# Feed-forward, up: eight products for the two leading chunks, two of five operand blocks made first

## The chip, the cores and the metric

The kernel runs on one core of one Trainium2 chip. The metric is the device time of one execution in microseconds (us); the median of three runs is compared. A core has TensorE (PE, matmuls out of SBUF into the PSUM banks), VectorE (DVE), ScalarE (ACT), GpSimd (POOL, which works on SBUF only here) and SyncE (SP, which issues the DMA transfers here). Each takes its instructions in a fixed order and waits for the others by semaphores.

## What is computed

Two transformer blocks in a row over 1024 tokens of width 1024, all in float32. The change is in the second block, between the output projection of its attention and the feed-forward part:

```python
x = x + gate1 * (merged @ w_out[i])
h2 = rmsnorm(x, g_ffn[i]) * (1 + scale2) + shift2
u = depthwise_conv_seq(h2 @ w_up[i], conv_w[i], conv_b[i])
u_val, u_gate = jnp.split(u, 2, axis=-1)
x = x + gate2 * ((jax.nn.gelu(u_gate, approximate=True) * u_val) @ w_down[i])
```

`w_up` has 1024 rows and 5632 columns, 2816 for `u_val` and 2816 for `u_gate`. `depthwise_conv_seq` has three taps along the tokens. `rmsnorm` needs the sum of squares of each token over all 1024 channels.

## The kernel before

Channels lie on the 128 partitions, tokens along the free dimension, in two halves of 512. Each float32 operand of a matmul is split into a high and a low part in a reduced format (`split_sb`: a copy on ACT makes the high part, a subtraction on DVE or POOL the low part), and a product takes three matmuls (high x high, high x low, low x high) for each block of 128 channels.

**Output projection.** `dense` goes over the tiles `mt` 0 to 7 in two groups of four, first token half, then second. `evac` (L1635) adds the residual (`stt` into `X3[th][:, mt]`), stores it, and `squares` adds up the squares in `acc[th]` (in the trace `ac`; `X3` and its slices are `x`, as is the residual's source). When the first half is complete (`after`, i = 12), `rstd_rows` makes the factor of each token: column sums by PE (`rs`), a power on POOL (`rbv`), transposes by PE (`rb`, a PSUM tile). The first half is then modulated and split into the operand blocks B11 (channels 0 to 511) and B21 (512 to 1023). When the second half is complete, a second `rstd_rows` (L1659) follows for `acc[1]`, out of the PSUM pool `o2ps`, which is then closed. The PSUM pool `upps` (six banks `u`) opens after it.

**Feed-forward, up.** There are 22 chunks `f`. Chunk f makes 128 channels of `u_val` (tile f) and 128 of `u_gate` (tile f + 22) for both token halves: a 2 x 2 by 2 x 2 block product. The weight blocks are a11, a12 (value, lower and upper channels) and a21, a22 (gate); the operand blocks B11, B21 (first token half) and B12, B22 (second). It is done with seven block products instead of eight, with sums of weight blocks (`weights`: `z` and `s4`, four DVE operations, split by `split_w`) and sums of operand blocks T1 = B12 - B11, T2 = B22 - T1, T3 = B12 - B22, T4 = T2 - B21. Each block product is 12 matmuls of 128x512 (`prod`, L1701 to L1707), a chunk 84. Then DVE adds the products together, ACT and DVE apply the taps, ACT the gelu, and the result goes to HBM (`a_d`).

The first two chunks are done together, since they come when T1, T2, T3, T4 and B22 are not there yet: `first` and `first2` for both (B11 and B21 products, 48 matmuls), then the loop over k = 0 to 3 (L1801 on), which modulates the second half and makes the five blocks for that k in one go, T1 and T3 and B22 with the low part on POOL, T2 and T4 on DVE, and then `up([0, 1])`, whose three first products go k by k. From chunk 2 on `up([f])` does one chunk after another.

**Order.** The program is written in the order of the source. A planner (a list scheduler with a model of the engines) then orders each engine's instructions: among those that are ready in its model it takes the one that stands first in the source. A PSUM bank or an SBUF tile is used again when its last reader is done. The pool `w2` (`a0`, `a1`, `r2`, `p5`, `cg`) takes the 32 KB per partition of X3[0] and, behind it, X3[1]; its tiles are laid out in the order of their first use in the source, in this kernel `p5`, `cg`, `a0`, `a1`, `r2`. The weights come by `raw` (L1671): tile f into `wst` (two buffers), tile f + 22 into `r2` (two buffers, trace name `r`), except for the first two chunks, where all come into `wst`. Split weights have four buffers (`wh`, `wl`).

Of the kernel before, what the change touches and what calls it, by code (L numbers as in the profile page):

```python
# [10 lines left out]
F32 = mybir.dt.float32  # L11
# [40 lines left out]
class Kernel:  # L52
# [1520 lines left out]
    def block2b(self):  # L1573
# [85 lines left out]
        rb = self.rstd_rows([acc[1]], D, 1e-6, t_, pp, "n", 2)  # L1659
# [11 lines left out]
        def raw(f, g, joint):  # L1671
            p, t = (w2, "r2") if g and not joint else (self.wp, "wst")
# [4 lines left out]
        def weights(f, joint):  # L1677
# [32 lines left out]
        P, P2 = {}, {}  # L1710
        K4 = range(4)

        def first(f, joint=False):

            gen = weights(f, joint)
            w = split_w(next(gen))
            a = bank()
            p1 = w1.tile([128, 512], F32, name="p1", tag="p1", bufs=2)
            cv = w1.tile([128, 1024], F32, name="cv", tag="cv", bufs=2)
            P[f] = gen, a, p1, cv, w  # L1720
            prod(a, w, 0, B11, K4, True)
            self.act(p1, a, AF.Copy)

        def first2(f, joint=False):
            gen, a, p1, cv, w = P[f]
            if joint:
                a = P2[f] = bank()
            prod(a, w, 1, B21, K4, joint)
            if not joint:
                self.act(cv[:, :512], a, AF.Copy)  # L1730

        W, b, c, d = {}, {}, {}, {}

        def up_weights(f):
            W[f] = [split_w(next(P[f][0])) for _ in range(2)]

        def up(fs):
            for f in fs:
                if f not in P:
                    first(f)  # L1740
            joint = len(fs) > 1
            for f in fs:
                if f not in W:
                    W[f] = [split_w(next(P[f][0]))]
                b[f] = bank()
                if not joint:
                    prod(b[f], W[f][0], 0, T2, K4, True)
                    first2(f)
                if len(W[f]) < 2:
                    W[f].append(split_w(next(P[f][0])))  # L1750
                c[f] = bank()
                if not joint:
                    prod(c[f], W[f][1], 0, T1, K4, True)
            if joint:
                for f in fs:
                    d[f] = bank()
                for k in K4:
                    for f in fs:
                        prod(b[f], W[f][0], 0, T2, [k], True)
                        prod(c[f], W[f][1], 0, T1, [k], True)  # L1760
                        prod(d[f], W[f][1], 1, T4, [k], True)
            for f in fs:
                gen, a, p1, cv, w = P.pop(f)
                if joint:
                    self.tt(cv[:, :512], p1, P2[f], ALU.add)
                self.tt(cv[:, 512:], p1, b[f], ALU.add)
                p5 = w2.tile([128, 512], F32, name="p5", tag="p5", bufs=2)
                self.act(p5, c[f], AF.Copy)
                cg = w2.tile([128, 1024], F32, name="cg", tag="cg", bufs=2)
                prod(b[f], W[f][0], 1, T3, K4, False)  # L1770
                self.tt(cg[:, 512:], p1, b[f], ALU.add)
                if not joint:
                    d[f] = bank()
                    prod(d[f], W[f][1], 1, T4, K4, True)
                self.tt(cg[:, :512], cg[:, 512:], d[f], ALU.subtract)
                self.tt(cg[:, 512:], cg[:, 512:], p5, ALU.add, eng=nc.gpsimd)
                w = split_w(next(gen))
                prod(c[f], w, 0, B22, K4, False)
                self.tt(cv[:, 512:], cv[:, 512:], c[f], ALU.add)
                a = []  # L1780
                for g, u in enumerate((cv, cg)):
                    mt = f + NFF * g
                    x = w2.tile([128, 1024], F32, name=f"a{g}", tag=f"a{g}", bufs=2 - g)
                    self.act(x, u, AF.Identity, bias=self.vec("conv_b", mt), scale=wc(1, mt))
                    self.stt(x[:, 1:], u[:, :1023], wc(0, mt), x[:, 1:], ALU.mult, ALU.add)
                    self.stt(x[:, :1023], u[:, 1:], wc(2, mt), x[:, :1023], ALU.mult, ALU.add)
                    a.append(x)
                self.act(a[1], a[1], AF.Gelu_apprx_tanh)
                self.tt(a[0], a[0], a[1], ALU.mult)
                nc.sync.dma_start(self.a_d[f], a[0])  # L1790


        db = w1.tile([128, 4], F32, name="db")
        self.tt(db, self.ada[:, 24:28], self.ada[:, 28:32], ALU.subtract)
        for f in range(2):
            first(f, True)
        for f in range(2):
            first2(f, True)
        for f in range(1):
            up_weights(f)  # L1800
        for k in range(4):  # L1801
            y11, y21, y12, y22 = (X3[th][:, k + 4 * i] for th in range(2) for i in range(2))
            modulate(y12, k, rb)
            modulate(y22, k + 4, rb)
            split = lambda y, b, e: self.split_sb(y, b[0][:, k], b[1][:, k], "a", e)
            b1, b2 = (self.ada[:, c:c + 1] for c in (24 + k, 28 + k))
# [12 lines left out]
        up([0, 1])  # L1819
        for f in range(2, NFF):  # L1820
            up([f])
# [10 lines left out]
        self.close(pp, w2, h0, w1, tp_)  # L1832
# [338 lines left out]
```

## Time and profile before

| | |
|---|---|
| time, three runs | 2283.76, 2284.2 and 2296.71 us, median 2284.2 |
| profiled execution | 2298.0 us, span 2296.1 us |
| granted TensorE clock, mean | 0.964 of full speed |
| busy share: PE, DVE, ACT, POOL | 93%, 66%, 42%, 50% |

The rows further down come from the profiled execution; their times are us from the start of its span. A row of a timeline gives the start, the duration, the engine, the source line (often that of a helper: L83 is any `tensor_tensor`, L86 any `scalar_tensor_tensor`, L102 any ACT operation, L111 the low part of a split, L1706 any matmul of the feed-forward up), the operation, the tile written and those read, and how many were merged into the row. Brackets give the time the engine stood idle before and what ended it.

### The profile page before, as it was taken

Reading aid. Unit: us, or ns where it says so; the run is one execution under the profiler, and the core shown is the slowest. Engines: PE = TensorE matmul, PEld = TensorE weight load, DVE = VectorE, ACT = ScalarE, POOL = GpSimd, SP = SyncE. Lnnn points to the kernel's source line nnn. Section 1 sums busy time; section 2 is a strip of 40 time slices with the busy share of each in tenths; the row PEclk is TensorE's granted clock in tenths of the full one; section 3 lists DMA queues with packets and bytes.
Section 4 is the critical chain, followed back from the end, with each engine's and each line's share of the span. In section 5 each row is a group of like instructions: output and inputs, shape, how many; then the busy total and the mean of one; then the engine's idle time right before and its main releaser. Section 6 shows DMA issues by size and latency. Waiting matters only on the chain. (4 is left out here: it accounts for less than half of the span.)

```text
span 2296.1 us, 29110 instructions
## 1 busy us (share of the span) xinstructions
PE 2130.7 (93%) x10192; PEld 1771.9 (77%) x10192; DVE 1523.6 (66%) x2522; ACT 972.5 (42%) x1717; POOL 1145.4 (50%) x738
## 2 busy tenths in 40 slices
PE   6998889899989989999999898997799999999998
PEld 4786777777877878888887786886678888877887
DVE  8969966652486245545656863437887777777676
ACT  4323345432246366657434443214444444455223
POOL 4725546665454455655323334515555555535471
PEclk8998999999999999999999999998899999999999
DMA  7433335555554656554345454542122222234332
GB/s 275 136 93 115 97 113 178 175 165 191 190 189 142 202 137 186 167 177 138 107 141 168 149 166 160 179 138 78 55 92 83 83 83 83 83 127 131 100 120 83
DMA packets 187261, 314.30 MB, mean 137 GB/s; under 512 B 43544, under 2 KB 85100, under 8 KB 187116
## 3 DMA queue, kind: packets, MB, share of 16 engines
q1 hardware_dynamic: 187116, 312.45, 42.6%
q8 instruction: 80, 1.31, 0.2%
q14 instruction: 65, 0.53, 0.1%
HBM read 226.70 MB, written 80.96 MB: 134 GB/s over the span
## 5 line engine op out<-in xcount | busy, mean ns | idle before, releaser
L111 POOL TENSOR_TENSOR wl<-wst,wh 128x1024 fp32r<-128x1024 f32 (+2 forms) x159 | 398.0, 2506 | 478.5 <-ACT wh L102 437.2
L102 ACT ACTIVATE wh<-wst 128x1024 fp32r<-128x1024 f32 (+1 forms) x164 | 168.3, 1028 | 270.1 <-PE ps L136 113.5
L83 POOL TENSOR_TENSOR acc<-acc,wa 128x512 f32<-128x512 f32 x84 | 108.9, 1296 | 16.7 <-ACT wa L102 13.3
L135 PE MATMUL ps<-xh,wh 128*128 128x512 f32 x256 | 104.0, 406 | 4.8 <-DVE kb L83 2.7
L137 PE MATMUL ps<-h0h,wl 128*128 128x512 f32 x256 | 104.1, 407 | 1.9 <-POOL wl L111 1.9
L135 PE MATMUL ps<-h0h,wh 128*128 128x512 f32 x256 | 104.5, 408 | 0.7 <-ACT wh L102 0.7
L135 PE MATMUL ps<-h1h,wh 128*128 128x512 f32 x256 | 101.8, 398 | 2.5 <-DVE qz L86 1.3
L136 PE MATMUL ps<-h0l,wh 128*128 128x512 f32 x256 | 103.6, 405 | 0.0
L83 POOL TENSOR_TENSOR tb<-rt,grid 128x384 f32<-128x384 f32 x48 | 43.1, 907 | 120.9 <-DVE mx L886 90.6
L136 PE MATMUL ps<-xl,wh 128*128 128x512 f32 x256 | 102.3, 400 | 0.0
L137 PE MATMUL ps<-xh,wl 128*128 128x512 f32 x256 | 102.3, 400 | 0.0
L136 PE MATMUL ps<-h1l,wh 128*128 128x512 f32 x256 | 102.0, 398 | 0.0
L137 PE MATMUL ps<-h1h,wl 128*128 128x512 f32 x256 | 101.4, 396 | 0.0
L135 PE MATMUL pd<-Ah,wh 128*128 128x512 f32 (+1 forms) x256 | 94.0, 367 | 5.3 <-ACT s L102 5.3
L136 PE MATMUL pd<-Al,wh 128*128 128x512 f32 (+1 forms) x256 | 93.9, 367 | 0.0
L137 PE MATMUL pd<-Ah,wl 128*128 128x512 f32 (+1 forms) x256 | 93.1, 367 | 0.0
L83 DVE TENSOR_TENSOR z<-r,wst 128x512 f32<-128x512 f32 x40 | 68.8, 1721 | 24.4 <-POOL wl L111 23.5
L90 POOL TENSOR_SCALAR wa<-wa,sc 128x512 f32<-128x512 f32 x36 | 58.9, 1635 | 49.3 <-DMA wa<-in_w_ada 48.4
L886 DVE CUSTOM_DVE_ANT_0 sp<-sp,tab 128x256 f32<-128x256 f32 (+1 forms) x128 | 52.7, 425 | 42.0 <-PE sp L163 27.4
L111 POOL TENSOR_TENSOR wl<-z,wh 128x1024 fp32r<-128x1024 f32 (+1 forms) x30 | 69.3, 2311 | 20.7 <-ACT wh L102 14.9
L102 ACT ACTIVATE a<-a 128x1024 f32<-128x1024 f32 x22 | 23.4, 1062 | 109.8 <-DVE a L86 109.8
L102 ACT ACTIVATE P<-sp,st 128x256 f32<-128x256 f32 (+1 forms) x128 | 59.1, 464 | 24.8 <-DVE st L886 23.4
(591 smaller groups left out, 7129.4 us busy)
## 6 DMA issues: line engine op xcount, KB each, us to landing
wa<-in_w_ada SPq DMA_DIRECT2D x96, 256.0 KB, 3.3
wst<-in_w_in SPq DMA_DIRECT2D x47, 512.0 KB, 3.8
wst<-in_w_up SPq DMA_DIRECT2D x26, 512.0 KB, 3.3
a_d<-a SPq DMA_DIRECT2D x22, 512.0 KB, 2.6
wst<-in_w_down SPq DMA_DIRECT2D x22, 512.0 KB, 3.6
as<-a_d SPq DMA_DIRECT2D x22, 512.0 KB, 3.9
r<-in_w_up SPq DMA_DIRECT2D x20, 512.0 KB, 3.2
wst<-in_w_out SPq DMA_DIRECT2D x16, 512.0 KB, 3.5
```

The source lines that it names most:

```text
L83: (eng or self.nc.vector).tensor_tensor(out, a, b, op)
L90: (eng or self.nc.vector).tensor_scalar(out, a, s1, None, op0=op0)
L102: self.nc.scalar.activation(out, a, f, **kw)
L111: self.last_lo = e.tensor_tensor(lo, y, hi.bitcast(F32), ALU.subtract)
L135: first = mm(ps, wh, xh, start=start, stop=False)
L136: mm(ps, wh, xl, start=False, stop=False)
L137: mm(ps, wl, xh, start=False, stop=stop)
L886: self.nc.vector.tensor_tensor_reduce(out=s, in0=s, in1=tab, scale=-1.0, scalar=-NEG, op0=ALU.add, op1=ALU.min, accum_out=m)
```

## The change

The first two chunks are computed with eight block products instead of seven, in another arrangement: for value and gate (g = 0, 1) the first token half is a1 B11 + a2 B21, and the second half is a1 B11 (kept as a copy `Q`) plus a1 T1 + a2 B22. So they need the weights as they come, no sums of them, and of the five operand blocks only T1 and B22. These two are made in a loop over k of their own, T1's low part now on DVE; T3, T2 and T4 follow in a second loop. T2, T3 and T4 are then first needed by chunk 2.

`begin(f)` makes the two B11 products of a chunk. `begin(0)` stands ahead of the second `rstd_rows`, `begin(1)` behind it; then the four B21 products. `acc[1]` and the small tile of `rstd_rows` move to a pool of their own (`na`), and `rs` and `rb` to a PSUM pool of their own (`nps`, two banks), which stays open until the end of the stage, so that `o2ps` closes without them. `up` is now written for one chunk, with the same products in the same order, and the taps are a function `conv`. `weights` issues both transfers of a chunk at once. `w2` opens where it did, but the convolutions of chunks 0 and 1 are now the first in the source to use it.

```diff
+        na, nps = self.open("nacc", "right"), self.open("nps", space=PSUM, bufs=2)
         t_, pp = self.open("o2"), self.open("o2ps", space=PSUM, bufs=4)
-        acc = [t_.tile([128, 512], F32, name=f"ac{i}") for i in range(2)]
+        acc = [p.tile([128, 512], F32, name=f"ac{i}") for i, p in enumerate((t_, na))]
...
-                rb = self.rstd_rows([acc[0]], D, 1e-6, t_, pp, "n", 2)
+                rb = self.rstd_rows([acc[0]], D, 1e-6, na, nps, "n", 2)
...
-        rb = self.rstd_rows([acc[1]], D, 1e-6, t_, pp, "n", 2)
         self.close(pp, t_, m_)
...
-            r1 = raw(f, 0, joint)
+            r1, r2 = raw(f, 0), raw(f, 1)
             yield r1
-            if joint:
-                r1 = raw(f, 0, joint)
-            r2 = raw(f, 1, joint)
...
+        W, Q, U = {}, {}, {}
+
+        def begin(f):
+            for g in range(2):
+                W[f, g] = split_w(raw(f, g, True))
+                U[f, g] = bank()
+                prod(U[f, g], W[f, g], 0, B11, K4, True)
+                Q[f, g] = w1.tile([128, 512], F32, name="q", tag=f"q{g}", bufs=2)
+                self.act(Q[f, g], U[f, g], AF.Copy)
+
+        begin(0)
+        rb = self.rstd_rows([acc[1]], D, 1e-6, na, nps, "n", 2)
+        begin(1)
+        C = {}
         for f in range(2):
-            first(f, True)
-        for f in range(2):
-            first2(f, True)
-        for f in range(1):
-            up_weights(f)
-        for k in range(4):
-            y11, y21, y12, y22 = (X3[th][:, k + 4 * i] for th in range(2) for i in range(2))
+            for g in range(2):
+                prod(U[f, g], W[f, g], 1, B21, K4, False)
+                C[f, g] = w1.tile([128, 1024], F32, name="c0", tag=("cv", "cg")[g], bufs=2)
+                self.act(C[f, g][:, :512], U[f, g], AF.Copy)
+        split = lambda y, k, b, e: self.split_sb(y, b[0][:, k], b[1][:, k], "a", e)
+        Y = lambda k: [X3[th][:, k + 4 * i] for th in range(2) for i in range(2)]
+        for k in K4:
+            y11, y21, y12, y22 = Y(k)
             modulate(y12, k, rb)
             modulate(y22, k + 4, rb)
...
-            self.act(y22, y22, AF.Identity, bias=b2)
-            self.stt(y11, y12, b1, y11, ALU.add, ALU.subtract)
-            self.stt(y12, y12, b1, y22, ALU.add, ALU.subtract)
-            split(y11, T1, "g")
-            split(y22, B22, "g")
+            self.act(y22, y22, AF.Identity, bias=self.ada[:, 28 + k:29 + k])
+            self.stt(y11, y12, self.ada[:, 24 + k:25 + k], y11, ALU.add, ALU.subtract)
+            split(y11, k, T1, "v")
+            split(y22, k, B22, "g")
+        for k in K4:
+            y11, y21, y12, y22 = Y(k)
+            self.stt(y12, y12, self.ada[:, 24 + k:25 + k], y22, ALU.add, ALU.subtract)
+            split(y12, k, T3, "g")
             self.tt(y22, y22, y11, ALU.subtract)
-            split(y22, T2, "v")
+            split(y22, k, T2, "v")
             self.tt(y21, y22, y21, ALU.subtract)
-            split(y21, T4, "v")
-            split(y12, T3, "g")
-        self.close(xp)
+            split(y21, k, T4, "v")
+        for f in range(2):
+            for g in range(2):
+                u = bank()
+                prod(u, W[f, g], 0, T1, K4, True)
+                prod(u, W[f, g], 1, B22, K4, False)
+                self.tt(C[f, g][:, 512:], Q[f, g], u, ALU.add)
+        self.close(na, xp)
         w2 = self.open("up2", "right")
-        up([0, 1])
+        for f in range(2):
+            conv(f, [C[f, g] for g in range(2)])
         for f in range(2, NFF):
-            up([f])
+            up(f)
```

## Rows read from the trace of the kernel before

**Rows 1.** Busy time by stretches: length, each engine (instructions), granted clock, DMA share, GB/s

```profile
1578.00:1653.00 75.00, 46.56 (x183) 37.29 (x182) 60.19 (x60) 31.23 (x48) 45.98 (x25) 0.80 0.15 56
1653.00:1672.00 19.00, 19.00 (x85) 15.49 (x84) 19.00 (x14) 8.83 (x10) 12.89 (x5) 1.00 0.15 56
1672.00:1700.00 28.00, 23.88 (x102) 18.45 (x101) 23.76 (x22) 13.42 (x15) 15.83 (x8) 1.00 0.26 95
1700.00:1750.00 50.00, 50.00 (x223) 41.39 (x222) 39.46 (x35) 20.81 (x26) 25.92 (x13) 1.00 0.22 82
```

**Rows 2.** Timeline of PE around the stretch

```profile
1577.93 0.39 PE L137 MATMUL ps<-mh,wl 128*128 128x512 f32 x1
...
1595.45 0.63 PE L1706 MATMUL u<-b11h,wl 128*128 128x512 f32 x1
1595.88 0.63 PE L1706 MATMUL u<-b11h,wh 128*128 128x512 f32 x1
...
1652.87 0.39 PE L1706 MATMUL u<-b11h,wh 128*128 128x512 f32 x1
...
1655.59 0.39 PE L1706 MATMUL u<-t2h,wh 128*128 128x512 f32 x1
```

**Rows 3.** Waits of PE, 1578 to 1653: us, times, longest

```profile
PE rs L199 <- DVE ac L83: 12.2, 1, 12.2
PE u L1706 <- ACT t2h L102: 9.4, 1, 9.4
PE u L1706 <- DVE t2l L111: 4.1, 1, 4.1
```

**Rows 4.** Timeline of DVE in the stretch

```profile
1577.34 0.67 DVE L83 TENSOR_TENSOR z<-wst 128x512 f32<-128x512 f32 x1
...
1578.55 0.68 DVE L83 TENSOR_TENSOR wst<-wst 128x512 f32<-128x512 f32 x1
1579.15 0.74 DVE L86 SCALAR_TENSOR_TENSOR x<-ps,ada,xr 128x512 f32<-128x512 f32 x1
1579.81 1.09 DVE L83 TENSOR_TENSOR z<-wst 128x512 f32<-128x512 f32 x1
...
1584.19 2.82 DVE L83 TENSOR_TENSOR s<-wst,z 128x512 f32<-128x512 f32 x1
...
1589.68 0.68 DVE L83 TENSOR_TENSOR ac<-ac,sq 128x512 f32<-128x512 f32 x1
...
1594.84 5.36 DVE L86 SCALAR_TENSOR_TENSOR x<-x,mods,rb 128x512 f32<-128x512 f32 x8 [2.30 <-PE rb L218]
...
1600.81 6.88 DVE L86 SCALAR_TENSOR_TENSOR x<-x,ada,x 128x512 f32<-128x512 f32 x4
...
1629.96 0.68 DVE L111 TENSOR_TENSOR t2l<-x,t2h 128x512 fp32r<-128x512 f32 x1
...
1632.37 1.28 DVE L111 TENSOR_TENSOR t4l<-x,t4h 128x512 fp32r<-128x512 f32 x2
...
1653.73 1.27 DVE L86 SCALAR_TENSOR_TENSOR a<-cg,vecs,a 128x1023 f32<-128x1023 f32 x1
```

**Rows 5.** Timeline of POOL

```profile
1586.43 2.78 POOL L111 TENSOR_TENSOR wl<-wst,wh 128x1024 fp32r<-128x1024 f32 x1
...
1603.70 6.81 POOL L111 TENSOR_TENSOR t1l<-x,t1h 128x512 fp32r<-128x512 f32 x4
...
1642.73 1.29 POOL L111 TENSOR_TENSOR wl<-s,wh 128x512 fp32r<-128x512 f32 x1 [0.81 <-ACT wh L102]
...
1649.72 2.41 POOL L111 TENSOR_TENSOR wl<-z,wh 128x1024 fp32r<-128x1024 f32 x1 [0.26 <-ACT wh L102]
```

**Rows 6.** The DMA queue of SP, and transfers by line (KB each, us to landing)

```profile
1630.67 0.80 SPq L1674 DMA_DIRECT2D r<-in_w_up  x2
...
r<-in_w_up SPq DMA_DIRECT2D x20, 512.0 KB, 3.2
```

**Rows 7.** Timeline of ACT

```profile
1648.59 1.06 ACT L102 ACTIVATE wh<-z 128x1024 fp32r<-128x1024 f32 x1 [2.84 <-PE u L1706]
```

More of the change, by code (lines that the diff above doesn't have):

```diff
@@ L1669, in block2b, with raw @@
         wc = lambda j, mt: self.vec("conv_w", 44 * j + mt)
-        def raw(f, g, joint):
-            p, t = (w2, "r2") if g and not joint else (self.wp, "wst")
+        def raw(f, g, early=False):
+            p, t = (w2, "r2") if g and not early else (self.wp, "wst")
             r = p.tile([128, 1024], F32, name=t, tag=t, bufs=2)
@@ L1709, in block2b, with conv @@
         bank = lambda: pp.tile([128, 512], F32, name="u", tag="u", bufs=6)
-        P, P2 = {}, {}
         K4 = range(4)
-        def first(f, joint=False):
-            gen = weights(f, joint)
+        def conv(f, us):
+            a = []
+            for g, u in enumerate(us):
+                mt = f + NFF * g
+                x = w2.tile([128, 1024], F32, name=f"a{g}", tag=f"a{g}", bufs=2 - g)
+                self.act(x, u, AF.Identity, bias=self.vec("conv_b", mt), scale=wc(1, mt))
+                self.stt(x[:, 1:], u[:, :1023], wc(0, mt), x[:, 1:], ALU.mult, ALU.add)
+                self.stt(x[:, :1023], u[:, 1:], wc(2, mt), x[:, :1023], ALU.mult, ALU.add)
+                a.append(x)
+            self.act(a[1], a[1], AF.Gelu_apprx_tanh)
+            self.tt(a[0], a[0], a[1], ALU.mult)
+            nc.sync.dma_start(self.a_d[f], a[0])
@@ L1716, in first, with up @@
+        def up(f):
+            gen = weights(f)
             w = split_w(next(gen))
             a = bank()
-            p1 = w1.tile([128, 512], F32, name="p1", tag="p1", bufs=2)
+            p1 = w1.tile([128, 512], F32, name="p1", tag="q0", bufs=2)
             cv = w1.tile([128, 1024], F32, name="cv", tag="cv", bufs=2)
-            P[f] = gen, a, p1, cv, w
             prod(a, w, 0, B11, K4, True)
             self.act(p1, a, AF.Copy)
[L1724 to L1790, printed above, removed]
@@ L1793, in block2b @@
-        db = w1.tile([128, 4], F32, name="db")
-        self.tt(db, self.ada[:, 24:28], self.ada[:, 28:32], ALU.subtract)
-        for f in range(2):
-            first(f, True)
-        for f in range(2):
-            first2(f, True)
-        for f in range(1):
-            up_weights(f)
-        for k in range(4):
-            y11, y21, y12, y22 = (X3[th][:, k + 4 * i] for th in range(2) for i in range(2))
+            w6 = split_w(next(gen))
+            b = bank()
+            prod(b, w6, 0, T2, K4, True)
@@ new lines, in up @@
+            prod(a, w, 1, B21, K4, False)
+            self.act(cv[:, :512], a, AF.Copy)
+            w5 = split_w(next(gen))
+            c = bank()
+            prod(c, w5, 0, T1, K4, True)
+            self.tt(cv[:, 512:], p1, b, ALU.add)
+            p5 = w2.tile([128, 512], F32, name="p5", tag="p5", bufs=2)
+            self.act(p5, c, AF.Copy)
+            cg = w2.tile([128, 1024], F32, name="cg", tag="cg", bufs=2)
+            prod(b, w6, 1, T3, K4, False)
+            self.tt(cg[:, 512:], p1, b, ALU.add)
@@ new lines, in up @@
+            d = bank()
+            prod(d, w5, 1, T4, K4, True)
+            self.tt(cg[:, :512], cg[:, 512:], d, ALU.subtract)
+            self.tt(cg[:, 512:], cg[:, 512:], p5, ALU.add, eng=nc.gpsimd)
+            w = split_w(next(gen))
+            prod(c, w, 0, B22, K4, False)
+            self.tt(cv[:, 512:], cv[:, 512:], c, ALU.add)
+            conv(f, (cv, cg))
+        W, Q, U = {}, {}, {}
[6 more added lines that the diff above has]
+                self.act(Q[f, g], U[f, g], AF.Copy)
@@ L1831, in block2b @@
             A[f] = [(hi[:, c:c + 512], lo[:, c:c + 512]) for c in (0, 512)]
-        self.close(pp, w2, h0, w1, tp_)
+        self.close(pp, nps, w2, h0, w1, tp_)
         ap_ = self.open("act")
```

4 lines of the change are left out of this document (1 added, 3 removed).

## The prediction

> **What bounds the kernel now.** I read first the busy time by stretches, then the waits of TensorE (PE) where it is not busy, then the order of the instructions on PE, VectorE (DVE), GpSimd (POOL) and the DMA queue there. In the steady chunk loop PE is busy all the time: 50.00 of 50 us, and 19.00 of 19 in chunk 2 [rows 1]. Matmuls of 128x512 follow each other every 0.2267 us: the twelve of chunk 2's B11 product go from 1652.87 to 1655.59 [rows 2]. So time is to be had only where PE stands still, and the change touches one such place: from 1578 to 1653 PE is busy 46.56 of 75 us, at a granted clock of 0.80, which is a mixture of its two levels; from 1672 to 1700 it misses another 4.1 us [rows 1]. The waits name the causes: 12.2 us for `ac` (the sum of squares of the second token half), 9.4 us for `t2h` and 4.1 us for `t2l`, operand blocks that DVE, ScalarE (ACT) and POOL make from it [rows 3]. After the first of these waits the matmuls are 0.43 us apart (1595.45 to 1595.88), as at 1.2 GHz [rows 2]; the timeline has some 20 such steps behind the three waits, worth 20 x 0.2 = 4 us.
>
> The stretch from the last matmul of the output projection (1577.93, so 1578.2 with its pitch) to chunk 2's first (1652.87) lasts 74.7 us [rows 2]. Its 168 matmuls need 168 x 0.2267 = 38.1. So 36.6 us are waits, slow clock, column sums and transposes.
>
> **The change, part by part.** I follow one mark, the start of chunk 2's T2 product: 1655.59 before [rows 2].
>
> *More matmuls.* Two chunks now take 2 x 96 = 192 instead of 168: 43.5 us, 5.4 more. Half of them (B11 and B21, 96, 21.8 us) need only the first token half; before, 48 did.
>
> *The start.* The first bank of the new `upps` still waits for the closing of `o2ps`, whose last reader is the evacuation at 1579.15 + 0.74 [rows 4]: PE starts at 1579.9. 24 matmuls (`begin(0)`) last to 1585.3. `rs` is behind them and needs `ac`. On DVE the four operations that combine chunk 0's weights fall away ahead of `ac`: 0.67 + 0.68 + 1.09 + 2.82 = 5.26 us, so `ac` (1589.68 + 0.68) ends at 1585.1 [rows 4]; I take 1586.0, because the last additions can still fall on a POOL subtraction. PE waits 0.7. If the planner left `rs` in front of `begin(0)`, as before, it would cost 2 to 4 us here, most of it hidden by the next step. From `ac`'s end to the first modulation took 1590.36 to 1594.84, 4.5 us [rows 4], so `rb` is usable at 1590.5. PE has 72 matmuls left (16.3 us) and about 2 us of column sums and transposes: it ends part one at 1604.3. The weights for `begin(1)` do not hold it up: before, the fourth weight split on POOL ended at 1586.43 + 2.78 = 1589.2 [rows 5], the third 2.7 us ahead of it, and PE, which resumes at about 1587, has twelve matmuls (2.7 us) for the third before it needs the fourth.
>
> *T1 and B22.* DVE: eight modulations, 5.36 us [rows 4], to 1595.9. Then four T1 differences and four T1 low parts, now on DVE (they were on POOL). A DVE operation of 128x512 takes 0.68 us alone (`t2l`) and 1.72 (6.88/4) beside POOL [rows 4]. Lower bound: eight alone, 5.4 us: 1601.3. Upper bound: the planner takes whatever is ready, and the four `y12` subtractions (second loop) are ready before the low parts, which must first wait for ACT; twelve at 1.72 is 20.6: 1616.5. Before, it put the four products of one level side by side in just this manner (x4, x8) [rows 4]. I take twelve, six beside POOL (two of the B22 and four of the T3 low parts), six alone: 6 x 1.72 + 6 x 0.68 = 14.4: T1 is complete at 1610.3. The first blocks are there by about 1604, so some nine matmuls run between the two times. Then 87 x 0.2267 = 19.7: PE ends both chunks at 1630.0. Bounds: 1604.3 + 21.8 = 1626.1, and 1616.5 + 19.7 + 1.5 for the low clock = 1637.7.
>
> *T2 and T4, now late.* The wait does not vanish, it moves to chunk 2. After T1 DVE still has 16 operations (10.9 us), one of them beside a POOL split of 2.78 (+2.1), and two additions into `c0` (1.4): T4 is complete at 1624.7. Chunk 2 needs T2 and the combined weights `z`, and these need `r2`. Before, the transfer of `r2` was issued at 1630.67, when the last `t2l`, the last reader of X3[1], had ended (1629.96 + 0.68), and not after the last `t4l` (1632.37 + 1.28) [rows 4, 6]: it lay in X3[1]. Now `a0` and `a1` are first used ahead of it, so it lies in X3[0], whose last reader is `t4l`. So the transfer leaves at 1624.7, lands 3.2 us later [rows 6] at 1627.9, and holds up what is queued behind it on SP (chunk 3's weights, not urgent). Then three additions for `z`, 2.0 us, but the convolutions of chunks 0 and 1 stand ahead of them by program order, eight operations of 1.27 us [rows 4]. None ahead: 0; all: 10.2. I take four (5.1), of which 1.9 pass while the transfer runs: 3.2. With 0.5 for handing over, `z` is done at 1633.6. Its high part takes 1.06 on ACT, its low part 2.41 on POOL [rows 5, 7]: 1637.3 with 0.2 between.
>
> *Sum.* PE is free for this product at 1630.0 + 2.7 = 1632.7 and begins it at 1637.3 instead of 1655.6: 18.3 us earlier. If the planner puts chunk 2's twelve B21 matmuls in front, 2.7 of the gap are used; if not, eight matmuls at the low clock cost 1.6: between them +0.5. DVE's backlog cost 4.1 us in 1672 to 1700 [rows 1]; six additions of the two chunks and the weight sums of chunk 1 are gone, and the gap gives DVE time: I take 2 of these us back. Gain 21 us.
>
> *At nothing.* ACT copies eight banks instead of four and splits four weight tiles instead of eight for the two chunks; it is busy 31 of 75 us there [rows 1], and would have to be late by the two or three us that T1's or T2's high parts leave it before this cost anything. Moving `acc[1]`, `rbv` and the two banks of `nps` only takes waits away. The loop from chunk 2 on does the same instructions.
>
> **Time.** The profiled execution has a span of 2296.1 us and was timed at 2298.0, 14 above the median of the three runs, 2284.2, but next to the slowest of them, 2296.7. The gain is a difference within the stretch, so I subtract it from the median: 2284 - 21 = 2263.
>
> **The rivals.**
> 1. *More.* The planner keeps T1's eight operations together and `z` ahead of the convolutions: T1 at 1601.3, both chunks done at 1626.1, T4 four `y12` operations (2.7) and 14.4 later, at 1618.4, `r2` at 1621.6, `z` split by 1628. PE then goes from chunk to chunk; the mark is at 1628.8: 26.8, and with 2 of the backlog 29: 2255. For it: T1 stands in a loop of its own. Against: the order by readiness in [rows 4]. Chance 0.21.
> 2. *The lock.* DVE and POOL take turns wholly. From 1590.5: 5.36 + 12 x 0.68 + 8 x 1.29 (a 512-wide subtraction on POOL alone [rows 5]) = 23.8: T1 at 1614.3, T4 at 1628.7; all eight convolution operations ahead of `z` (8.3 after the landing): mark at 1646, slow start 1.6: gain 8, 2276. For it: `t1l` takes 6.81/4 = 1.70 on POOL while DVE's operations take 1.72, one for one [rows 4, 5]. Against: 0.68 + 1.29 = 1.97, so they overlap by a quarter of a microsecond. Chance 0.20. The Trainium skill (SBUF — State Buffer, Who interferes with whom) has this rule: a DVE instruction with two SBUF inputs and a GpSimd instruction that reads SBUF shut each other out for the whole instruction. The trace agrees in the pattern, not to the full length; by the rule alone the time would be this rival's.
> 3. *Slower.* One mechanism: SP's queue in the chunk loop. `weights` now issues `r2` together with `r1`; `r2`'s buffer is free only when the split of two chunks before is done, and a waiting transfer holds up the next `wst` and the stores of `a_d`. If that delays each chunk's first split, PE waits in each of 20 chunks: at 1.05 us a chunk the gain is gone, at 2.2 the kernel is 1% slower. Against: PE misses nothing there now, and DVE has 10.5 of 50 us free [rows 1], 4 per chunk. Chance 0.06.
>
> **How the numbers follow.** My forecast has 0.53, by itself 2258 to 2270. A measurement of this kernel can tell about 1%, 22.8 us, from no change: that is 2261.4. Faster by more: rival 1 (0.21) and a good third of the forecast (0.19), 0.40. Within 1%: the rest of the forecast and rival 2, 0.54. Slower: rival 3, 0.06. The range that takes in rivals 1 and 2: 2255 to 2276.
>
> **What would show it.** Right: no wait of PE for `ac` above 2 us; a single gap of at most 6 us before the T1 products; chunk 2's first matmul about 23 us earlier; `r2` issued at the end of the last `t4l`; a gap of some 5 us before chunk 2's T2. Wrong: `rs` still ahead of the B11 products; T1's low parts behind T3's or T2's work; `z` of chunk 2 before any convolution or behind all; PE waits after chunk 4.

## The result and the profile after

The changed kernel takes 2266.69 us (median of four runs, 2264.16 to 2267.92), against 2288.43 us of the kernel before, measured beside it; the ratio is 0.9899 with a 95% interval of 0.9872 to 0.9927. That is 23 us of 2288 (the two medians lie 21.7 apart). A ratio of 1 lies outside the interval, but the interval reaches to both sides of 1%, which the prediction took as the least that a measurement of this kernel can tell.

Two more measures are used below, both from the profiled execution. The *stage* goes from the end of the last output-projection matmul to the start of the first matmul of the feed-forward down: 461.05 us before, 440.28 after, so 20.8 us. *To the end* goes on to the end of the span: 717.9 and 696.3, 21.6 us. Times written with a + count from the end of the last output-projection matmul. The spans themselves (2296.1 and 2263.5) differ by 32.6; the remaining 10.9 us lie ahead of the stage, where TensorE has the same instructions in the same order in both programs. There the output projection ends at 1578.2 in the one and at 1567.2 in the other, and in the other kernels below, whose TensorE work is alike up to there too, anywhere between 1566.9 and 1575.6. So this part is taken as variation between executions and not as gain.

The busy time by stretches of the kernel after (columns as in [rows 1]); the first stretch is the output projection's end to chunk 2's first T2 matmul:

```profile
1567.20:1626.30 59.10, 51.52 (x217) 40.99 (x216) 51.05 (x59) 32.63 (x50) 25.05 (x15) 0.94 0.13 45
1672.00:1700.00 28.00, 28.00 (x125) 23.18 (x125) 21.10 (x20) 12.48 (x15) 13.88 (x7) 1.00 0.21 75
1700.00:1750.00 50.00, 50.00 (x222) 41.43 (x221) 39.61 (x35) 21.77 (x25) 29.54 (x14) 1.00 0.23 85
```

PE is busy 51.5 of 59.1 us where it had 46.56 of 75 [rows 1], at a granted clock of 0.94 instead of 0.80. From 1672 to 1700, where it missed 4.1 us, it misses nothing; the same part of the program now lies some 30 us earlier, and there its one wait is 0.8 us, for `cv` at 1640.64. The chunk loop is full as before. The waits of PE in the stage of the kernel after (us, times, longest):

```profile
PE u L1704 <- DVE t1l L111: 3.9, 1, 3.9
PE u L1704 <- ACT wh L102: 2.7, 1, 2.7
PE u L1704 <- DVE cv L83: 0.8, 1, 0.8
PE rs L199 <- DVE ac L83: 0.6, 1, 0.6
```

The 12.2 us for `ac` have become 0.6, the 9.4 and 4.1 for T2 [rows 3] are gone, and two new ones, 3.9 for T1's low part and 2.7 for chunk 2's weights, have come. The timeline of PE, as in [rows 2], shows where:

```profile
1567.01 0.39 PE L137 MATMUL ps<-mh,wl 128*128 128x512 f32 x1
1567.24 0.39 PE L1704 MATMUL u<-b11h,wh 128*128 128x512 f32 x1
...
1577.33 1.02 PE L199 MATMUL rs<-ones_d,ac 128*128 128x1 f32 x8 [0.59 <-DVE ac L83]
...
1584.01 0.60 PE L218 MATMUL rb<-ident,rbv 128*128 128x128 f32 x4
...
1597.08 0.80 PE L1704 MATMUL u<-t1l,wh 128*128 128x512 f32 x1 [3.95 <-DVE t1l L111]
1597.67 0.63 PE L1704 MATMUL u<-t1h,wl 128*128 128x512 f32 x1
1598.10 0.63 PE L1704 MATMUL u<-t1h,wh 128*128 128x512 f32 x1
...
1620.81 0.39 PE L1704 MATMUL u<-b11h,wh 128*128 128x512 f32 x1
...
1626.36 0.50 PE L1704 MATMUL u<-t2h,wh 128*128 128x512 f32 x1 [2.67 <-ACT wh L102]
```

The first B11 matmul follows the last of the output projection without a gap. The steps of 0.43 us (1597.67 to 1598.10) are 1.2 GHz again: the granted clock is 1.00 from 1590 to 1596.1, into the 3.95 us of standing still, 0.50 from 1596.2 to 1602.9, over twelve such steps, and 1.00 again up to the wait of 2.67, behind which it is 0.50 from 1626.9 to 1630.2. DVE in the same stretch, as in [rows 4]:

```profile
1575.41 1.77 DVE L83 TENSOR_TENSOR ac<-ac,sq 128x512 f32<-128x512 f32 x1
...
1584.64 5.36 DVE L86 SCALAR_TENSOR_TENSOR x<-x,mods,rb 128x512 f32<-128x512 f32 x8 [6.09 <-PE rb L218]
1589.92 5.18 DVE L86 SCALAR_TENSOR_TENSOR x<-x,ada,x 128x512 f32<-128x512 f32 x4
1595.02 1.40 DVE L86 SCALAR_TENSOR_TENSOR x<-x,ada 128x512 f32<-128x512 f32 x2
1596.34 0.68 DVE L111 TENSOR_TENSOR t1l<-x,t1h 128x512 fp32r<-128x512 f32 x1
...
1604.91 0.68 DVE L111 TENSOR_TENSOR t1l<-x,t1h 128x512 fp32r<-128x512 f32 x1
...
1611.53 2.49 DVE L111 TENSOR_TENSOR t4l<-x,t4h 128x512 fp32r<-128x512 f32 x4
...
1615.99 1.38 DVE L86 SCALAR_TENSOR_TENSOR a<-c,vecs,a 128x1023 f32<-128x1023 f32 x1 [0.64 <-ACT a L102]
1617.43 0.69 DVE L83 TENSOR_TENSOR z<-r,wst 128x512 f32<-128x512 f32 x1
1618.04 2.47 DVE L86 SCALAR_TENSOR_TENSOR a<-c,vecs,a 128x1023 f32<-128x1023 f32 x2
...
1622.82 0.69 DVE L83 TENSOR_TENSOR z<-r,wst 128x512 f32<-128x512 f32 x1
```

and POOL (as in [rows 5]), ACT (as in [rows 7]) and the queue of SP (as in [rows 6]) beside it:

```profile
1578.63 1.01 POOL L206 TENSOR_TENSOR rbv<-rbv,mhalf 128x4 f32<-128x4 f32 x1 [2.00 <-DVE rbv L205]
...
1596.50 6.73 POOL L111 TENSOR_TENSOR t3l<-x,t3h 128x512 fp32r<-128x512 f32 x4 [2.61 <-ACT t3h L102]
...
1626.39 2.88 POOL L111 TENSOR_TENSOR wl<-z,wh 128x1024 fp32r<-128x1024 f32 x1 [10.10 <-ACT wh L102]
```

```profile
1623.01 1.28 ACT L102 ACT_TABLE_LOAD   x1
1624.31 1.06 ACT L102 ACTIVATE a<-a 128x1024 f32<-128x1024 f32 x1
1625.27 1.04 ACT L102 ACTIVATE wh<-z 128x1024 fp32r<-128x1024 f32 x1
...
1614.05 0.81 SPq L1675 DMA_DIRECT2D r<-in_w_up  x2
```

Four things can be read here. DVE stood idle for 6.09 us before the modulations, waiting for `rb`; but `rbv`, all that the transposes need, was ready at 1578.63 + 1.01 = 1579.64, and PE came to them only at 1584.01, after the rest of `begin(1)` and fifteen B21 matmuls. T1's low parts stand between the `y12` subtractions of the second loop (`x<-x,ada`). The transfer of `r2` leaves right behind the last `t4l` (1611.53 + 2.49 = 1614.02). And `wh<-z` stands behind the load of the gelu's table and the gelu.

### The profile page after: what moved, and what is told of

It is laid out like the page before. It is cut to its first block, busy times and chain, and to the rows that moved or that the text cites. A ratio compares the mean times of both kernels' runs of the same rounds, so it can differ in the third digit from the quotient of the medians.

```text
span 2263.5 us, 29117 instructions
## 1 busy us (share of the span) xinstructions
PE 2122.7 (94%) x10216; PEld 1766.0 (78%) x10216; DVE 1502.9 (66%) x2511; ACT 969.7 (43%) x1717; POOL 1124.1 (50%) x728
## 4 chain that ended last, share of the span: by engine, by line
PE 41%; DVE 6%; DMA 2%; issue 1%; ACT 1%; POOL 1%; SPq 0%; POOLq 0%; DVEq 0%; ACTq 0%
PE u L1704 17%; PE ps L137 4%; PE ps L135 4%; PE ps L136 4%; PE pd L1885 3%; PE pd L136 2%; PE pd L135 2%; PE pd L137 2%; PE po L1386 1%; DMA ox<-o_d 1%; DVE P L90 1%; PE tp L1378 1%; DVE x L86 1%; DMA as<-a_d 1%; DVE a L86 1%
## 5 line engine op out<-in xcount | busy, mean ns | idle before, releaser
L111 POOL TENSOR_TENSOR wl<-z,wh 128x1024 fp32r<-128x1024 f32 (+1 forms) x28 | 63.9, 2282 | 30.8 <-ACT wh L102 27.2
L83 DVE TENSOR_TENSOR s<-s,pd 128x512 f32<-128x512 f32 x76 | 51.0, 681 | 27.9 <-PE pd L137 14.1
```

The lines of the kernel that those rows point to most:

```text
L83: (eng or self.nc.vector).tensor_tensor(out, a, b, op)
L111: self.last_lo = e.tensor_tensor(lo, y, hi.bitcast(F32), ALU.subtract)
```

## The experiments

Theory A: the gain is the time that the 48 more matmuls which need only the first token half cover, and what is left comes from one chain (`ac`, `rb`, T1, T4, `r2`, `z`) whose links can be shortened. Rival B: the start alone (pools and order around `ac`) does it, the waits being independent. Rival C came up on the way: the end of the chain is DVE's and ACT's work on the convolutions of chunks 0 and 1.

All kernels but the first are the changed one with the edits named. The table gives, from the profiled execution, the stage, the time to the end, all waits of PE in the stage added up, and what the slow steps cost (steps of 0.3 to 0.5 us between matmuls, each less 0.2267), and the ratio of the times to those of the kernel before, measured beside each.

| kernel | stage | to the end | PE waits | slow steps | ratio |
|---|---|---|---|---|---|
| before | 461.1 | 717.9 | 32.7 | 4.2 | |
| after | 440.3 | 696.3 | 8.4 | 4.2 | 0.9899 (0.9872 to 0.9927) |
| start_only | 462.6 | 718.8 | 31.9 | 6.6 | 1.0009 (0.9995 to 1.0022) |
| eight_only | 445.4 | 698.5 | 14.7 | 2.4 | 0.9924 (0.9909 to 0.9939) |
| r2_wst | 437.2 | 693.2 | 7.9 | 1.9 | 0.9902 (0.9879 to 0.9925) |
| rb_early | 437.4 | 695.5 | 7.3 | 3.0 | 0.9902 (0.9888 to 0.9917) |
| t1_pool | 441.3 | 694.0 | 10.4 | 2.6 | 0.9918 (0.9894 to 0.9941) |
| t1_low_first | 445.8 | 701.5 | 13.7 | 3.7 | 0.9934 (0.9911 to 0.9956) |
| rb_r2 | 438.4 | 694.7 | 7.1 | 3.9 | 0.9898 (0.9877 to 0.9920) |
| all3 | 438.1 | 694.6 | 8.2 | 3.1 | 0.9908 (0.9887 to 0.9928) |
| sums_back | 440.6 | 697.3 | 9.5 | 4.0 | 0.9927 (0.9907 to 0.9947) |
| r2_late1 | 444.6 | 696.3 | 12.0 | 5.0 | 0.9899 (0.9881 to 0.9918) |
| rb_r2_late1 | 442.4 | 698.0 | 11.7 | 2.8 | 0.9923 (0.9906 to 0.9939) |
| rb_r2_no_taps | 433.2 | 689.2 | 4.5 | 2.1 | 0.9875 (0.9855 to 0.9895) |

The columns account for each stage: with 1848 matmuls of 0.2267 us before (418.9) and 1872 after (424.4), 2 to 5 us are left over in every row. Two cautions: a stage is one execution, and the feed-forward down, the same work in all, takes 251.7 to 258.1 us, so a gain of 3 us in the stage need not reach the end. Total times can't tell such differences: 3 us are 0.13%, and the intervals are some 0.3% or more wide.

### The start alone

The kernel before with `na` and `nps` and the second `rstd_rows` between the first two chunks' B11 and B21 work, still seven products.

```diff
...
-        for f in range(2):
-            first(f, True)
+        first(0, True)
+        rb = self.rstd_rows([acc[1]], D, 1e-6, na, nps, "n", 2)
+        first(1, True)
```

> The kernel before with seven products, and only the small tiles of the second rstd_rows (rs, rb, acc[1]) in pools of their own, so that the B11 and B21 products of both chunks no longer stand behind rb on PE. I measure from the last matmul of the output projection to the last matmul of the feed-forward up: 461.0 us before, 440.2 after. Theory A (the chain ac, rb, modulations, T blocks on DVE sets when PE goes on; matmuls pulled ahead of it fill a hole that opens again behind them): rb comes no earlier than before, since the weight sums still stand ahead of ac on DVE, so the 12.2 us wait only changes its name and joins the wait for T2: 459 to 461 us, no gain beyond 2. Rival B (the waits add up, each is removed by itself): the 12.2 us wait and its slow clock go: 447 to 449 us.

Its waits of PE, the longest two:

```profile
PE u L1706 <- ACT t2h L102: 23.2, 1, 23.2
PE u L1706 <- DVE b21l L111: 4.2, 1, 4.2
```

The wait for `ac` is gone and nothing is gained: 462.6 us, 1.6 above A's range and 13.6 or more above B's. The 12.2, 9.4 and 4.1 us of [rows 3] were one chain seen at three places; PE goes ahead sooner, runs out of matmuls that need only the first token half, and waits at `t2h` for all of it. B falls. One thing is not separated here: the transposes `rb` now stand behind matmuls on PE, so that the modulations start at +21.1 instead of +16.7. T4 is complete no later for it (+55.0, and +55.5 before), but the start with `rb` kept early was not tried on seven products.

### Eight products without the new start

The changed kernel with `rs` and `rb` back in `o2ps` and the second `rstd_rows` in front of `begin(0)`.

```diff
-        na, nps = self.open("nacc", "right"), self.open("nps", space=PSUM, bufs=2)
...
+        rb = self.rstd_rows([acc[1]], D, 1e-6, t_, pp, "n", 2)
         self.close(pp, t_, m_)
...
         begin(0)
-        rb = self.rstd_rows([acc[1]], D, 1e-6, na, nps, "n", 2)
         begin(1)
...
```

> The changed kernel with rs and rb back in the pool o2ps, so that PE makes rs and rb before any B11 product; eight products, T1 and B22 first, as in the change. Theory A: ac is as early as in the change and rb does not stand behind B21 matmuls, so the modulations start about 3 us earlier than in the change; PE starts its 96 matmuls at about +14.5 us instead of at once, T1 is ready before they end, both chunks are done at +58 to +60 instead of +53.6, but chunk 2's weights are then ready in time: 441 to 444 us from the last projection matmul to the last of the feed-forward up (440.2 in the change, 461.0 before). Rival B (waits add up): the wait for ac is back in full, 12 us and its slow clock: 452 to 455 us.

```profile
PE rs L199 <- DVE ac L83: 9.8, 1, 9.8
PE u L1704 <- ACT q L102: 3.0, 3, 1.6
```

These are its two longest waits of PE. The stage is 445.4, 1.4 above A's range and 6.6 below B's: without the new start the change brings 15.7 of the 20.8 us. The start brings 5.1 on top in the stage (2.2 to the end), and nothing without the rest. The 15.7 us belong to the eight products and to the loop that makes only T1 and B22 first, together: the products use that order, and no run parts the 48 more matmuls of the first token half from the later need for T2, T3 and T4. That these matmuls are what covers the time, as A has it, is argued from the waits: the 9.4 and 4.1 us for T2 are gone. The waits for T1 and for chunk 2's weights are not there, where PE comes to them later by the 9.8 us and DVE earlier (T4 is complete at +43.3, in the changed kernel at +46.8).

### Which link of the chain is worth what

**Weight sums.** The four DVE operations on chunk 0's weights put back, unused.

```diff
...
+            if f == 0:
+                z = w1.tile([128, 1024], F32, name="z", tag="z")
+                s4 = w1.tile([128, 512], F32, name="s4", tag="s4", bufs=2)
...
+                self.tt(z[:, 512:], a21, a11, ALU.subtract)
+                self.tt(z[:, :512], a21, a22, ALU.add)
+                self.tt(z[:, :512], z[:, :512], a11, ALU.subtract)
+                self.tt(s4, a12, z[:, :512], ALU.subtract)
...
```

> The changed kernel with the four VectorE operations on chunk 0's weight tiles (the sums of weight blocks that nine... seven products needed) put back into their buffers, where nothing reads them. Measure: last output-projection matmul to last up matmul, 440.3 in the changed kernel. Theory A (the start is set by the rb transposes that stand behind fifteen B21 matmuls on TensorE; VectorE waits for rb anyway): 440.0 to 442, mods still start 17 to 18 us behind the last output-projection matmul. Rival (it is the fewer weight sums that let the start go sooner): ac or the bank evictions move back by the 5 us of these four operations, 444 to 446.

The modulations start at +17.4, as in the changed kernel, and the stage is 440.6, as A expected. The four operations run at 1534.65 to 1537.87, as soon as the two tiles have landed, for 0.69 us each, 34 us ahead of the output projection's end. So the sums can stay without cost, if they run as soon as their tiles are there. Where they stood before, directly ahead of `ac`, this run does not tell what they cost, but the others do: `ac` ends at +12.2 and +12.3 with the sums there (before, `start_only`), and at +9.8 to +10.0 in all kernels without them there. That is some 2.4 us and not the 5.26 that the prediction took off: without the sums, other DVE operations fall on POOL's splits, as a low part of B11 here, in the kernel before and then in the one after:

```profile
1576.08 0.68 DVE L111 TENSOR_TENSOR b11l<-x,b11h 128x512 fp32r<-128x512 f32 x1
...
1565.16 2.84 DVE L111 TENSOR_TENSOR b11l<-x,b11h 128x512 fp32r<-128x512 f32 x1
```

In the changed kernel and in `sums_back`, what the modulations wait for is `rb` on PE:

```profile
1580.44 1.77 DVE L83 TENSOR_TENSOR ac<-ac,sq 128x512 f32<-128x512 f32 x1
1583.42 0.16 DVE L205 TENSOR_SCALAR rbv<-rs 128x4 f32<-128x4 f32 x1 [1.21 <-PE rs L199]
1589.68 2.72 DVE L86 SCALAR_TENSOR_TENSOR x<-x,mods,rb 128x512 f32<-128x512 f32 x4 [6.09 <-PE rb L218]
```

This is DVE's timeline of `sums_back`: `ac`'s last addition directly followed by `rbv`, and the same idle 6.09 us.

**The transposes.** The B21 matmuls of chunk 0 ordered behind the `rb` transposes on PE.

```diff
...
+        tr = self.chain[-1]
         begin(1)
...
-                prod(U[f, g], W[f, g], 1, B21, K4, False)
+                prod(U[f, g], W[f, g], 1, B21, K4, False, tr)
```

> The changed kernel with an order on PE: the B21 products behind the transposes rb, which in the change stand behind 15 of these matmuls although the power on POOL has been done for 4.4 us. Theory A: the modulations start 3.4 us earlier, and with them all of the T blocks; the wait for T1 (3.9 us) shrinks to about 0.5 and its slow clock (2.6) goes, the wait at chunk 2 grows by the difference: 436 to 438 us instead of 440.2. Rival B: all of 6 us comes through: 434 to 435 us. Rival C (DVE's backlog): the gain is what DVE starts earlier, 3.4, or less when it waits later: 437 to 440 us.

The timeline of DVE and the longest wait of PE in this kernel:

```profile
1585.35 5.36 DVE L86 SCALAR_TENSOR_TENSOR x<-x,mods,rb 128x512 f32<-128x512 f32 x8 [2.71 <-PE rb L218]
```

```profile
PE u L1704 <- ACT wh L102: 4.8, 1, 4.8
```

The modulations start at +14.0, 3.4 us sooner, T1 and T4 are 3.1 sooner; the wait for T1 falls from 3.9 to 1.5 (A expected 0.5). Two of these three us come back as a longer wait for chunk 2's weights. The stage is 437.4, in A's range (436 to 438) and in C's (437 to 440), so this run does not tell the two apart.

**Chunk 2's second weight tile.** Into the free buffer of `wst`, so that it need not wait for X3[0].

```diff
-            r1, r2 = raw(f, 0), raw(f, 1)
+            r1, r2 = raw(f, 0), raw(f, 1, f == 2)
```

> The changed kernel with one difference: chunk 2's second weight tile is loaded into the buffer wst instead of r2, so that it need not wait for the last T4 block. Theory A: the three additions for z run in DVE's idle time before rb, the wait at chunk 2 (2.7 us), its eight matmuls at the low clock (1.6) and the reordering behind it go: 435 to 437 us instead of 440.2. Rival C (DVE's backlog of convolutions sets the pace of chunks 2 and 3): the wait comes back at chunk 3 for its own z: 439 to 440.5 us.

The stage is 437.2, at the upper end of A's 435 to 437. Chunk 2's weight sums move into DVE's idle time before `rb` and the wait for `wh` is gone; in its place stand 2.0 us for `p`. The sum of waits falls by only 0.5 us, the slow steps by 2.3. Of these 2.3, some 1.0 are the slow steps that stood behind the wait for `wh`; the two waits for `p` (1.16 and 0.83 us) have one step of 0.34 each behind them. For the rest, some 1.3, the trace shows no cause in the edit: ahead of T1's low part PE stands still for the same time in both kernels, 3.95 and 3.96 us, but the slow steps behind it cost 2.5 us in the changed kernel and 1.1 here. The stretches at the low clock (columns as in [rows 1]), of the changed kernel and of `r2_wst`:

```profile
1596.20:1602.90 6.70, 5.83 (x14) 4.47 (x15) 6.70 (x6) 2.11 (x4) 6.40 (x4) 0.50 0.00 0
...
1600.10:1603.40 3.30, 2.93 (x7) 2.35 (x8) 3.30 (x3) 1.01 (x2) 3.30 (x3) 0.50 0.00 0
```

So a stage can differ by a microsecond or more through the clock alone, and of the 3.1 us some 1.8 can be put down to the edit.

**Both.** `rb_r2` has these last two edits.

> Both of rb_early and r2_wst on the changed kernel: B21 behind rb on PE, and chunk 2's second weight tile in wst. Theory A (two waits, the first for T1 through rb, the second for chunk 2's weights, the second of which grows when the first shrinks): the gains add up and the 2 us by which the wait at chunk 2 grew are saved too: 432 to 435 us (440.2 in the change, 437.2 and 437.4 with one of them). Rival C (DVE's backlog): not below 436.

**T1's low part.** Back on POOL:

```diff
-            split(y11, k, T1, "v")
+            split(y11, k, T1, "g")
```

> The changed kernel with the low part of T1 on POOL again, as before the change. Theory A with the take-turns reading of DVE and POOL: T1's low parts follow B22's on POOL at 1.3 to 1.7 us each and are complete some 3 us earlier than in the change (+35 instead of +38.4 us after the last projection matmul); DVE has four operations fewer but shares its reads with POOL longer, T4 is complete at +45 to +48 (+46.8 in the change). The wait for T1 stays at 2 to 4 us: 438 to 441 us from the last projection matmul to the last of the feed-forward up (440.2 in the change). Rival (POOL's lock dominates): T4 later than +49 and the stage longer than 442.

And with the `y12` subtractions of the second loop held behind T1's last low part:

```diff
+            lo = self.last_lo
...
-            self.stt(y12, y12, self.ada[:, 24 + k:25 + k], y22, ALU.add, ALU.subtract)
+            self.after(lo, nc.vector.scalar_tensor_tensor(y12, y12, self.ada[:, 24 + k:25 + k], y22,
+                                                          op0=ALU.add, op1=ALU.subtract))
```

> The changed kernel with the four y12 subtractions held behind T1's last low part on DVE. Theory A: T1 is complete at +31 to +33 us instead of +38.4, but its first low part comes only 1 us earlier, and the wait of PE is for the first: 3.9 becomes 2.5 to 3; T3, T2 and T4 end where they did, the wait at chunk 2 grows by about a microsecond: 439 to 441 us (440.2 in the change). Rival (the wait is for T1 as a whole, as the prediction counted it): 435 to 437.

**All three.** 

> rb_r2, and the y12 subtractions held behind T1's last low part. Theory A: what is left of the wait for T1 (1.5 us with rb early) goes, T4 may come a little later, which nothing waits for now: 431 to 434 us. Rival C: not below 436.

With the low part on POOL the stage is 1 us longer (441.3, between what A and its rival expected; T4 is done 1.9 us later and the wait for `wh` grows to 5.5), but the time to the end is 2.3 shorter, so that it is a matter of one or two us either way. T1 first is a miss: T1 is complete 8.1 us sooner (+30.3 instead of +38.4), yet the stage is 5.5 us longer. T4 comes 2.3 later, six of the eight convolution operations instead of four stand ahead of the last addition for chunk 2's `z`, and `z` is done at +62.0 instead of +56.3; chunk 2's T2 product starts at +66.6 instead of +59.1, and ahead of it PE stands still for 7.1 us at `p`. So T1 isn't what the end waits for. `rb_r2` (438.4, expected 432 to 435) and `all3` (438.1, expected 431 to 434) miss too. Gains of 2.8 and 3.1 do not add up. Part of that is the clock: less their slow steps, the stages are 436.1 (after), 435.3 (`r2_wst`), 434.4 (`rb_early`) and 434.5 (`rb_r2`): gains of 0.8 and 1.7, and 1.6 for both. Even so they don't add up, so something else, too, holds the stage at about 438.

### What holds it at 438

In `rb_r2`, DVE's timeline from T4 on, and PE's waits:

```profile
1618.10 8.09 DVE L86 SCALAR_TENSOR_TENSOR a<-c,vecs,a 128x1023 f32<-128x1023 f32 x3 [0.59 <-ACT a L102]
...
1634.87 0.68 DVE L83 TENSOR_TENSOR s<-wst,z 128x512 f32<-128x512 f32 x1
```

```profile
PE u L1704 <- DVE t1l L111: 2.6, 1, 2.6
PE u L1704 <- ACT p L102: 2.4, 2, 2.2
```

Three convolution operations take 8.09 us here, beside POOL's splits of weights (2.68 and 3.39 us, from 1619.10 on), where one alone takes 1.27 [rows 4], and the sums of chunk 3's weights end after 1635. So the next kernel, `rb_r2` otherwise, leaves out the two outer taps of the convolution in chunks 0 and 1, eight DVE operations (that part of the computation is missing in it); two others, on `r2_wst` and on `rb_r2`, have chunk 1's convolution behind chunk 2's products. Rival D: the floor is made of the waits for `ac` and T1 and of slow steps, and the waits for `p` only change name.

```diff
...
-                self.stt(x[:, 1:], u[:, :1023], wc(0, mt), x[:, 1:], ALU.mult, ALU.add)
-                self.stt(x[:, :1023], u[:, 1:], wc(2, mt), x[:, :1023], ALU.mult, ALU.add)
+                if f > 1:
+                    self.stt(x[:, 1:], u[:, :1023], wc(0, mt), x[:, 1:], ALU.mult, ALU.add)
+                    self.stt(x[:, :1023], u[:, 1:], wc(2, mt), x[:, :1023], ALU.mult, ALU.add)
```

> The kernel with both repairs (B21 behind the rb transposes, chunk 2's second weight tile in the free buffer), with the two outer taps of the convolution left out for chunks 0 and 1, which is eight scalar_tensor_tensor operations of VectorE less; it leaves out this part of the computation. Theory C: the wait for p (2.4 us of 438.4) goes, 434.5 to 436.5. Rival D: 437.5 to 439.

```diff
-        for f in range(2):
-            conv(f, [C[f, g] for g in range(2)])
-        for f in range(2, NFF):
+        conv(0, [C[0, g] for g in range(2)])
+        up(2)
+        conv(1, [C[1, g] for g in range(2)])
+        for f in range(3, NFF):
             up(f)
```

> The changed kernel with chunk 2's second weight tile in the free wst buffer, and with the convolution of chunk 1 put behind chunk 2's products in the program. Theory C (a floor of 437 to 438 is left because VectorE and ScalarE work off the convolutions of chunks 0 and 1 while chunk 2 wants its operands and PSUM tiles): the wait for p (2.0 us) goes, 434.5 to 436. Rival D (the floor is made of the first wait for ac, the wait for the first T1 block and steps at the low granted clock; the waits for p only change name): 437 or more.

> As r2_late1, with the B21 matmuls of chunk 0 held behind the rb transposes on TensorE as well. Theory C: 433.5 to 436, and no wait for p over 0.5 us. Rival D: 437 or more, the waits only change name.

Without the taps the stage is 433.2, below what C expected (434.5 to 436.5) and well below D's 437.5 to 439; the sum for chunk 3 starts at

```profile
1629.02 0.69 DVE L83 TENSOR_TENSOR s<-wst,z 128x512 f32<-128x512 f32 x1
```

and of the waits for `p` 0.3 us are left. The 5.2 us are 2.1 of that wait, 0.5 for `cv`, 1.8 of slow steps, and 0.8 of what the columns don't hold; 3.4 are left without the slow steps, and the time to the end is 5.5 shorter. So the DVE work of the two first convolutions does hold back the stage, which is C, as far as one execution shows it; the ratios of the two kernels (0.9875 and 0.9898) have intervals that overlap.

Putting it off does not help. With chunk 1's convolution behind chunk 2 the waits for `p` grow instead, as in `rb_r2_late1`:

```profile
PE u L1704 <- ACT p L102: 6.4, 3, 3.1
PE u L1704 <- DVE cg L83: 1.5, 1, 1.5
```

C expected 433.5 to 436, and it is 442.4; in `r2_late1` C expected 434.5 to 436, and it is 444.6: the stage is longer than without the move, though in total time the difference is not clear. D's "437 or more" takes both in, but its account does not, since the waits for `p` grow. The edit also changed PE's order (chunk 2's T3 and T4 products moved among the others). For the longest of the three waits, 3.13 us up to 1627.35, the timeline of ACT in `rb_r2_late1` shows what stands ahead:

```profile
1624.46 1.28 ACT L102 ACT_TABLE_LOAD   x1 [7.45 <-DVE a L86]
...
1626.72 0.58 ACT L102 ACTIVATE p<-u 128x512 f32<-128x512 f32 x1
```

ACT takes `p` only behind the gelu of chunk 0, and this waits for the taps of chunk 0 on DVE, which the edit left where they were: `p` is done at +60.4, and at +59.9 in `rb_r2`, where PE comes to it later and waits 0.26. So what is new in this wait is PE's order. What makes the two others is open. No version that computes all is faster than the changed kernel by more than the totals can tell.

## Why the prediction was right, step by step

Times with a + count from 1578.2 before and from 1567.24 after. The gain of 21 us was 20.8 in the stage and 21.6 to the end; the mark, chunk 2's T2 product, was forecast at +59.1 and came at +59.1. That it agreed so closely is partly luck: steps on the way were missed by 2 to 6 us in both directions.

- **The start, wrong by 1.7 us.** PE was to wait for the closing of `o2ps` (+1.7). It goes straight on (1567.24). `ac` then ended at +9.9 instead of +7.8. The sum took 5.26 us off for the four weight sums and gave 0.9 back for one collision with POOL; in fact the last addition took 1.77 us instead of 0.68, as allowed for, but a low part of B11 took 2.84 instead of 0.68 as well. PE's wait for `ac`, forecast 0.7, is 0.6.
- **`rb`, the mis-sized step: +17.4 instead of +12.3.** Of these 5.1 us, 2.1 are `ac`'s. The prediction took the 4.5 us from `ac` to the first modulation over from [rows 4]; they became 7.5. There PE had nothing else to do. Now the transposes share PE with matmuls that the planner had put in front: the sum needed the place of `rb` in PE's order. `rb_early` shows it: placed sooner, modulations at +14.0, 4.1 us behind `ac`.
- **T1, length nearly right, place wrong.** Twelve operations by readiness, forecast 14.4 us. From 1589.92 to 1605.59, 15.7 us, DVE does these twelve, with the `y12` subtractions between the low parts as forecast, and two T2 differences as well (1.76 and 0.68 us). With `rb` late T1 is complete at +38.4 instead of +32.1. It matters little: PE starts with the first block and waits once, 3.9 us (forecast: a gap of at most 6), and both chunks are done at +53.6 instead of +51.8.
- **T4, right by a second error: +46.8 against +46.5.** The 14.4 us between T1 and T4 (16 operations, one collision, two additions into `c0`) were 8.4. Two of the 16 had run inside T1's stretch, the other 14 follow each other every 0.6 us, POOL has no work from 1603.2 to 1612.4, and the additions into `c0` come after T4. This gives back the 6 us that `rb` and T1 had lost.
- **`r2` and `z`, right.** The transfer leaves behind the last `t4l`, as the layout of `w2` said, and `z` is done at +56.3 (+55.4), with four of the eight convolution operations ahead of its last addition, as forecast.
- **`z` to the mark, right by a third pair.** Not seen: the load of the gelu's table (1.28 us) and the gelu (1.06) in front of `wh<-z`, so that it starts 1.76 us behind `z` instead of 0.2. Also not seen: the first T2 matmuls take only the high part of the weights, so PE doesn't wait for POOL's 2.88 us, and it fills in products of T1, T4 and B21. PE's wait is 2.67 us where 4.6 were forecast.
- **After the mark, right in sum.** Forecast 2 us of DVE's backlog and 0.5: of the 4.1 us of 1672 to 1700 only the 0.8 for `cv` are left, and some 2 us go to slow steps behind the wait of 2.67 (the nine steps from 1626.36 to 1630.39 take 4.03 us).
- **The rivals.** *More* did not come: the low parts of T1 were not kept together; and `t1_low_first` shows that its first half would not have helped. *The lock* overstates, though DVE is slowed as it said: [rows 4] had 1.72 us beside POOL; after, DVE's operations take 1.73 to 1.77 (two `x<-x,ada` in 3.46 us, a `t1l` in 1.77) while POOL's four `t3l` take 6.73/4 = 1.68. The Trainium skill (SBUF — State Buffer, Who interferes with whom) would have the one wait for the whole of the other; alone they take 0.68 + 1.29 = 1.97, and a pair takes 1.7, so here too the rule holds in the pattern and not to the full length. *Slower* did not come: PE is busy 50.00 of 50 us in the loop, with `r2` issued early.

## What to carry to other kernels

Waits of one engine behind one late value are one chain, not a list: take one away and the time comes back at the next, until there is work that needs nothing of the chain; here that work (eight products, with T2, T3 and T4 needed later) was worth 15.7 us of the stage, and the earlier start only something together with it. When an instruction moves to a new place in an engine's order, cost it by what now stands ahead of it there: here PE came to four small transposes 4.4 us after they could have run, which no duration showed. And when repairs that each seem to give three us do not add up, take the slow steps out of each first, and then look for the work that is behind all of them, by leaving it out for one run.

## What was not expected of the hardware

- What a wait costs in slow steps behind it can't be read off its length. The same wait of 3.95 us was followed by 2.5 us of slow steps in the changed kernel, where the granted clock was 0.50 up to 1602.9, and by 1.1 in `r2_wst`, where PE went on at 1600.47 and the clock was 1.00 again from 1603.5. A wait of 2.67 us was followed by seven slow steps in the changed kernel; one of 2.65 in `t1_low_first` by a single one, at a granted clock of 1.00 from 1599.9 to 1603.0.
- The output projection, on TensorE the same in all these programs, ended between 1566.9 and 1578.2 us after the start of the span in fourteen executions. Two spans of single executions are no measure of a change of 20 us; the difference between two points within the execution is.
- The load of an activation table took 1.28 us, directly between two other ACT operations (1623.01 to 1624.31), and fell in front of a weight split that PE was waiting for. The Trainium skill (ScalarE: Activation LUTs, What ACT_TABLE_LOAD costs) gives 1283 ns for the load, which this row agrees with, and about as much again for a drain, of which this place shows none: the operation ahead of it ended at 1621.75 + 1.24 = 1622.99.
